# Two decoder layers on one core: the columns of two neighbouring 64-byte lines in turn on TensorE's moving side

## The chip, the cores and the metric

One core of one Trainium2 chip. The time is that of one execution on the device in microseconds; a single core runs, so it is its own slowest.

## The reference

An input x of 256 tokens by 2048 features goes through two pre-norm residual layers in float32. Cut to what matters here:

```
def layer_a(x):                        # latent attention, 16 heads
    h = rms_norm(x, norm_a)
    proj = h @ w_in                    # 2048 -> 512 + 256 + 64 (latents) + 2048 (gate)
    q  = rms_norm(q_lat)  @ w_q_up     # 512 -> 16 x 192
    kv = rms_norm(kv_lat) @ w_kv_up    # 256 -> 16 x (128 + 128)
    o = causal_attention(q, k, v)      # norms on q and k, rotary part of 64
    return x + (o * silu(gate)) @ w_out

def layer_b(x):                        # block attention; with 256 tokens one block of 256
    q, k, v, gate = split(rms_norm(x, norm_b) @ w_in, 4)     # 2048 -> 4 x 2048
    o = causal_attention(rms_norm(q), rms_norm(k), v, alibi) # 16 heads of 128
    return x + (o * silu(gate)) @ w_out
```

## The kernel before

Features lie on the 128 partitions, so `xT` and the residual `xt` are [128, 16 chunks, 256 tokens]. Every dense product is made of three passes in float32r: an operand is cut into a high part (rounded to float32r) and the low rest, and high x high, high x low and low x high are added up in PSUM (`acc`, five banks of 512 columns; attention works in the other three).

Weights stream from DRAM once, in chunks of 128 rows. `W.load` brings a chunk into `wr`; `W.split` makes its parts, `wh` by a ScalarE copy (L124) and `wl` by a VectorE subtraction (L125), 528 splits in all, mostly of 512 columns.

There are two kinds of dense product. `blk_rows` has the tokens as the stationary operand (128 x 128) and the weight as the moving one, 384, 416 or 512 columns: it makes the latents, q, k and v. `blk_cols` has 128 columns of the weight as the stationary operand and all 256 tokens as the moving one: it makes the gates and both output products. Each matmul brings its own load of 128 x 128 stationary values. In attention, `products` makes the scores (`ps_s`), and `s3` in `head_steps` makes the value product (`ps_o`): v stationary, the transposed softmax weights `ph`, `pl`, `p1` moving. Its result times the gate is `og`, cut into `ogh` and `ogl`, the moving side of the output products.

TensorE's work is a written list: `ordered` puts steps of attention between the chunks of dense products by assumed costs, and `chain` keeps TensorE in that order. `run` issues loads and splits four chunks ahead. `xh` and `xl` are the parts of the normed input; `token_scale` makes the norm's factor per token, as a column and (by a product of `ones` with a diagonal tile) along rows; `out_done_a` and `out_done_b` add `acc` to the residual. `flip` transposes q, k and the softmax weights through a DMA: its copies read every second 16-bit word of a tile, or write so.

A row of a tile stands in one partition, 4 bytes for a column. All tiles named here start at a multiple of 64 bytes, so 16 neighbouring columns are one line of 64 bytes in this text.

Of the kernel before, what the change touches and what calls it, by code (L numbers as in the profile page):

```python
"""Two decoder layers (latent attention, then block-sparse attention) on one core.

The dense products run as three float32r passes over operands split exactly into a high and a
low part of 12 bits each. Activations are kept with features on partitions, so that no layer
boundary needs a transpose; weights stream from DRAM once.
"""
# [9 lines left out]
F32 = mybir.dt.float32  # L16
# [5 lines left out]
ALU = mybir.AluOpType  # L22
# [7 lines left out]
WARM = 34  # products of ones while the first loads run  # L30
ACC = 5  # PSUM banks that gather products over the chunks of a weight; attention works in the others
HALF = 3  # chunks of a gate's block that come before the next projections

# tiles for: loaded chunks of weights, their parts; chunks loaded and split ahead
# [3 lines left out]
# For the order of the work, in ns: how long after the end of a piece on the tensor engine what  # L38
# it leaves is ready (norms of the projections of layer a and b, latents, transposed q and k,
# scores, transposed weights of attention of both layers, output of a head), times SLACK; how long  # L40
# a bank is held; and how far pieces of attention lie apart.
# [12 lines left out]
# columns of the packed gains  # L54
# [3 lines left out]
# columns of the packed constants of shape  # L58
# [10 lines left out]
]  # L69


@with_exitstack
def trunk(ctx: ExitStack, tc, xT, gains, cst, w_in_a, w_q_up, w_kv_up, w_out_a, w_in_b, w_out_b, outT):
# [15 lines left out]
    def cut(t, *sizes):  # L89
        """Pieces of a tile, one after the other, each [P, a, b]."""  # L90
        out, at = [], 0
        for a, b in sizes:
            out.append(t[:, at:at + a * b].rearrange("p (a b) -> p a b", a=a))
            at += a * b
        return out
# [4 lines left out]
    # ---------------------------------------------------------------- weights  # L100
    class W:
        """Chunks of 128 rows of a weight, [rows, n] in DRAM, and their high and low parts."""

        def __init__(self, src):
            self.before = lambda: None
            self.src, self.kc, self.n = src, src.shape[0] // P, src.shape[1]
            self.per = max(1, 512 // self.n)
            self.h, self.l = {}, {}
# [10 lines left out]
        def split(self, c):  # L119
            """The parts of the chunks from c on, as many as there are in one step."""  # L120
# [3 lines left out]
            nc.scalar.activation(h, raw, AF.Copy)  # L124
            nc.vector.tensor_tensor(l, raw, h.bitcast(F32), op=ALU.subtract)  # L125
# [3 lines left out]
    # ---------------------------------------------------------------- order of the work  # L129
    class Step:  # L130
        """A piece of work of the tensor engine: about cost ns there, and lag ns from its end until
        what it leaves can be used; needs what some steps leave, and comes after others."""
# [10 lines left out]
    def ordered(main, side):  # L143
        """Steps of main in their order; those of side come between, each as soon as it can and
        one of the three banks that they work in is free."""
# [20 lines left out]
    def chain(ins):  # L166
        """Keep the tensor engine's work in the order in which it is written."""
# [11 lines left out]
    def blk_rows(w, x, done, lag=PB, first=()):  # L179
        """out[token, n] = x.T w for w [K, n]: tokens stationary, the weight streams."""  # L180
# [3 lines left out]
        def go(wt, c, k):  # L184
# [3 lines left out]
            for t in range(2):  # L188
                ts = slice(t * P, (t + 1) * P)
                o = a[t][:, :n]  # L190
                matmul(o, xh[:, k, ts], wt.h[c], start=k == 0, stop=False)
                matmul(o, xh[:, k, ts], wt.l[c], start=False, stop=False)
                matmul(o, xl[:, k, ts], wt.h[c], start=False, stop=k == nk - 1)
# [3 lines left out]
        return _steps(w, go, 6 * (n / 2.4 + 2.5), lag, first)  # L197

    def blk_cols(w, x, done, lag=3000):
        """out[n, token] = w.T x for w [K, n]: the weight stationary, tokens stream."""  # L200
# [3 lines left out]
        def go(wt, c, k):  # L204
# [3 lines left out]
            for s in range(ns):  # L208
# [4 lines left out]
                matmul(o, wt.h[c][:, ws], xh[:, k], start=first, stop=False)  # L213
                matmul(o, wt.h[c][:, ws], xl[:, k], start=False, stop=False)
                matmul(o, wt.l[c][:, ws], xh[:, k], start=False, stop=last)
# [5 lines left out]
    def _steps(w, go, cost, lag, first=()):  # L221
# [3 lines left out]
        for n in list(first) + [nc_w] * nk:  # L225
# [3 lines left out]
            wt = W(w[k0 * P:k1 * P])  # L229
# [21 lines left out]
    # ---------------------------------------------------------------- small things  # L251
    g_sb = one.tile([P, G_END], F32, name="g_sb")
# [18 lines left out]
    def rsqrt(v, n, tag):  # L271
        """v ** -0.5 for positive v: a first guess by its bits, then Newton's steps."""
# [16 lines left out]
    def after(ins, prior):  # L289
        """Work of one engine in this order."""  # L290
# [3 lines left out]
    def sum_squares(ssq, j):  # L294
        """ssq[feature, token] gathers the squares of the two chunks of features j."""
# [9 lines left out]
    def token_scale(ssq, lay, out, needs, more):  # L305
        """1 / rms of each token: as a column per half of the tokens, and along rows."""
# [10 lines left out]
        def g():  # L317
# [4 lines left out]
            matmul(pr[:, :S], ones, d, start=True, stop=True)  # L322
# [6 lines left out]
    # ---------------------------------------------------------------- gates  # L329
# [572 lines left out]
```

## Time and profile before

| | |
|---|---|
| median of 3 runs | 783.33 us (783.16 to 785.5) |
| span of the profiled execution | 780.9 us |
| TensorE busy | 772.9 us, 99% |
| TensorE's weight loads | 717.7 us, 92% |
| VectorE busy | 602.7 us, 77% |
| ScalarE busy | 512.3 us, 66% |
| HBM | 182 GB/s over the span |

The span runs from the first to the last instruction of the profiled execution; the runs' time holds some 2.4 us more. PE is TensorE's matmuls, PEld its loads of stationary operands (they overlap), DVE VectorE, ACT ScalarE. Busy time of PE is not a measure of its speed, since the matmuls are pipelined and their ends are modelled; the distance from one start to the next is.

### The profile page before, as it was taken

How to read it: one execution, taken by the hardware profiler on the slowest of the kernel's cores; microseconds unless marked ns; L12 is line 12 of the kernel's file. 1: busy time of each engine (PE TensorE's matmuls, PEld its weight loads, DVE VectorE, ACT ScalarE, POOL GpSimd, SP SyncE). 2: the span in 40 equal slices, each digit the busy share in tenths (PEclk: the TensorE clock that was granted, in tenths of full speed). 3: DMA queues.
4: the chain of work that ended last, by engine and by line, in shares of the span. 5: the costliest groups of instructions: out<-in, count | busy, mean ns of one | idle time of the engine just before them, and what ended most of it. 6: DMA issues, size and time to landing. Idle time of an engine off the chain costs nothing.

```text
span 780.9 us, 14905 instructions
## 1 busy us (share of the span) xinstructions
PE 772.9 (99%) x5246; PEld 717.7 (92%) x5246; DVE 602.7 (77%) x1470; ACT 512.3 (66%) x1288; POOL 0.2 (0%) x4
## 2 busy tenths in 40 slices
PE   8999999999999999999999999999999999999997
PEld 8999999999999999988889888898889988899997
DVE  7888899999987787766787777786687957887553
ACT  7677898888877665545666556665567655675442
POOL 0000000000000000000000000000000000000000
PEclk9999999999999999999999999999999999999999
DMA  9765656666559766766777667776777677767871
GB/s 305 234 179 174 169 159 182 180 161 158 167 166 249 233 195 188 207 179 183 214 217 175 211 182 222 216 199 191 186 223 208 186 210 194 214 192 213 252 213 61
DMA packets 137979, 153.24 MB, mean 196 GB/s; under 512 B 47280, under 2 KB 94768, under 8 KB 137904
## 3 DMA queue, kind: packets, MB, share of 16 engines
q1 hardware_dynamic: 137760, 152.27, 69.1%
q8 instruction: 41, 0.67, 0.4%
q14 instruction: 34, 0.28, 0.1%
q10 hardware_dynamic: 144, 0.02, 0.0%
HBM read 139.68 MB, written 2.10 MB: 182 GB/s over the span
## 4 chain that ended last, share of the span: by engine, by line
PE 97%; DMA 2%; DVE 1%; SPq 0%; issue 0%; ACT 0%
PE acc L174 89%; PE ps_s L174 4%; PE ps_o L174 2%; PE ps_ta L177 1%; DMA sm<-pz 1%; DMA wr<-w_in_a 1%; DVE wl L125 0%; PE ps_lt L177 0%; DVE xt L825 0%; PE ps_st L174 0%; SPq L449 0%; PE ps_r L174 0%; SPq L113 0%; ACT wh L124 0%; PE ps_kr L177 0%
## 5 line engine op out<-in xcount | busy, mean ns | idle before, releaser
L124 ACT ACTIVATE wh<-wr 128x512 fp32r<-128x512 f32 (+2 forms) x528 | 320.9, 618 | 193.0 <-PE acc L174 120.9
L125 DVE TENSOR_TENSOR wl<-wr,wh 128x512 fp32r<-128x512 f32 (+2 forms) x528 | 348.4, 673 | 109.2 <-ACT wh L124 102.7
L174 PE MATMUL acc<-wh,xh 128*128 128x512 f32 (+1 forms) x448 | 173.8, 388 | 0.8 <-ACT wh L124 0.8
L174 PE MATMUL acc<-wl,xh 128*128 128x512 f32 (+1 forms) x448 | 173.9, 388 | 0.3 <-DVE wl L125 0.3
L174 PE MATMUL acc<-wh,xl 128*128 128x512 f32 (+1 forms) x448 | 174.2, 389 | 0.0
L174 PE MATMUL acc<-xh,wh 128*128 128x256 f32 x512 | 143.8, 281 | 0.0
L174 PE MATMUL acc<-ogh,wh 128*128 128x256 f32 x512 | 142.6, 279 | 0.0
L174 PE MATMUL acc<-xh,wl 128*128 128x256 f32 x512 | 142.3, 278 | 0.2 <-DVE wl L125 0.2
L174 PE MATMUL acc<-xl,wh 128*128 128x256 f32 x512 | 142.3, 278 | 0.0
L174 PE MATMUL acc<-ogl,wh 128*128 128x256 f32 x512 | 141.6, 277 | 0.0
L174 PE MATMUL acc<-ogh,wl 128*128 128x256 f32 x512 | 141.5, 276 | 0.0
L174 PEld LDWEIGHTS acc<-wh,xh 128*128 128x128 f32 x448 | 84.5, 189 | 17.4 <-ACT wh L124 1.5
L174 PEld LDWEIGHTS acc<-wl,xh 128*128 128x128 f32 x448 | 84.4, 188 | 17.4 <-DVE wl L125 0.9
L174 PEld LDWEIGHTS acc<-wh,xl 128*128 128x128 f32 x448 | 84.5, 189 | 15.1
L174 PEld LDWEIGHTS acc<-xl,wh 128*128 128x128 f32 x512 | 96.6, 189 | 0.2
L174 PEld LDWEIGHTS acc<-xh,wl 128*128 128x128 f32 x512 | 96.3, 188 | 0.4 <-DVE wl L125 0.4
L174 PEld LDWEIGHTS acc<-xh,wh 128*128 128x128 f32 x512 | 96.2, 188 | 0.2
L174 PEld LDWEIGHTS acc<-ogh,wh 128*128 128x128 f32 x512 | 96.3, 188 | 0.0
L174 PEld LDWEIGHTS acc<-ogl,wh 128*128 128x128 f32 x512 | 96.2, 188 | 0.0
L174 PEld LDWEIGHTS acc<-ogh,wl 128*128 128x128 f32 x512 | 96.1, 188 | 0.0
L174 PE MATMUL acc<-wh,xt 128*128 128x384 f32 (+1 forms) x192 | 59.5, 367 | 0.0
L174 PEld LDWEIGHTS acc<-wh,xt 128*128 128x128 f32 x192 | 35.5, 188 | 2.1
(150 smaller groups left out, 824.0 us busy)
## 6 DMA issues: line engine op xcount, KB each, us to landing
wr<-w_in_b SPq DMA_DIRECT2D x128, 512.0 KB, 4.2
wr<-w_in_a SPq DMA_DIRECT2D x32, 512.0 KB, 4.6
wr<-w_out_a SPq DMA_DIRECT2D x32, 512.0 KB, 4.5
wr<-w_out_b SPq DMA_DIRECT2D x32, 512.0 KB, 4.5
wr<-w_in_a SPq DMA_DIRECT2D x15, 416.0 KB, 5.0
wr<-w_q_up SPq DMA_DIRECT2D x16, 384.0 KB, 3.4
wr<-w_kv_up SPq DMA_DIRECT2D x8, 512.0 KB, 3.7
xt<-xT SPq DMA_DIRECT2D x4, 512.0 KB, 6.0
```

The lines of the kernel that those rows point to most:

```text
L124: nc.scalar.activation(h, raw, AF.Copy)
L125: nc.vector.tensor_tensor(l, raw, h.bitcast(F32), op=ALU.subtract)
L174: chain(nc.tensor.matmul(*args, skip_group_check=True, **kw))
L177: chain(nc.tensor.transpose(*args))
```

## The change

The moving operand of a product is read in another order. `paired` views 32 columns as two lines of 16 and takes a column of the one and of the other in turn: 0, 16, 1, 17, ... 15, 31, then the next 32. Where the moving operand is a weight (`blk_rows`), its parts are stored so that this order gives the columns as they were: `unpaired` reads `raw` as 0, 2, 4, ... 30, 1, 3, ... 31, so with a step of two columns, and the parts are written line after line. Where the moving operand is the tokens, results come out with the tokens in the paired order and stay so (gates, the row of norm factors, `og`); `ogh`, `ogl` and the residual get the natural order back by an `unpaired` read of `og` and `acc`. The scores' products are left as they are. `g_sb` is allocated with 320 columns instead of 298, which moves all tiles behind it by 64 bytes. No engine has an instruction more or less, and their order is the same.

```
+def paired(v):
+    return v.rearrange("p (g l e) -> p g e l", l=2, e=16)
+def lines(v):
+    return v.rearrange("p (g l e) -> p g l e", l=2, e=16)
+def unpaired(v):
+    return v.rearrange("p (g e l) -> p g l e", l=2, e=16)
...
         def split(self, c):
             m = min(self.per, self.kc - c)
             h, l = self.part("wh", F32R, m, NH, 512), self.part("wl", F32R, m, NH, 512)
             raw = self.raw[:, c:c + m]
-            nc.scalar.activation(h, raw, AF.Copy)
-            nc.vector.tensor_tensor(l, raw, h.bitcast(F32), op=ALU.subtract)
+            ho, lo = h, l
+            if self.moving:
+                assert m == 1
+                raw, ho, lo = unpaired(raw[:, 0]), lines(h[:, 0]), lines(l[:, 0])
+            nc.scalar.activation(ho, raw, AF.Copy)
+            nc.vector.tensor_tensor(lo, raw, ho.bitcast(F32), op=ALU.subtract)
...
     def blk_rows(w, x, done, lag=PB, first=()):
-                matmul(o, xh[:, k, ts], wt.h[c], start=k == 0, stop=False)
-                matmul(o, xh[:, k, ts], wt.l[c], start=False, stop=False)
-                matmul(o, xl[:, k, ts], wt.h[c], start=False, stop=k == nk - 1)
+                matmul(o, xh[:, k, ts], paired(wt.h[c]), start=k == 0, stop=False)
+                matmul(o, xh[:, k, ts], paired(wt.l[c]), start=False, stop=False)
+                matmul(o, xl[:, k, ts], paired(wt.h[c]), start=False, stop=k == nk - 1)
...
     def blk_cols(w, x, done, lag=3000):
-                matmul(o, wt.h[c][:, ws], xh[:, k], start=first, stop=False)
-                matmul(o, wt.h[c][:, ws], xl[:, k], start=False, stop=False)
-                matmul(o, wt.l[c][:, ws], xh[:, k], start=False, stop=last)
+                matmul(o, wt.h[c][:, ws], paired(xh[:, k]), start=first, stop=False)
+                matmul(o, wt.h[c][:, ws], paired(xl[:, k]), start=False, stop=False)
+                matmul(o, wt.l[c][:, ws], paired(xh[:, k]), start=False, stop=last)
...
-    g_sb = one.tile([P, G_END], F32, name="g_sb")
+    g_sb = one.tile([P, 320], F32, name="g_sb")
...
-            matmul(pr[:, :S], ones, d, start=True, stop=True)
+            matmul(pr[:, :S], ones, paired(d), start=True, stop=True)
...
         def s3():
-            matmul(po[:, :S], vh, ph, start=True, stop=False)
-            matmul(po[:, :S], vh, pl, start=False, stop=False)
-            matmul(po[:, :S], vl, ph, start=False, stop=False)
-            matmul(po[:, P:S], v1, p1, start=False, stop=True)
+            matmul(po[:, :S], vh, paired(ph), start=True, stop=False)
+            matmul(po[:, :S], vh, paired(pl), start=False, stop=False)
+            matmul(po[:, :S], vl, paired(ph), start=False, stop=False)
+            matmul(po[:, P:S], v1, paired(p1), start=False, stop=True)
...
-            nc.scalar.activation(ogh[:, h], og, AF.Copy)
-            nc.vector.tensor_tensor(ogl[:, h], og, ogh[:, h].bitcast(F32), op=ALU.subtract)
+            nc.scalar.activation(lines(ogh[:, h]), unpaired(og), AF.Copy)
+            nc.vector.tensor_tensor(lines(ogl[:, h]), unpaired(og), lines(ogh[:, h].bitcast(F32)), op=ALU.subtract)
...
     def out_done_a(j):
-            both = xt[:, c:c + 2].rearrange("p a b -> p (a b)")
-            nc.vector.tensor_tensor(both, a[0], both, op=ALU.add)
+            both = lines(xt[:, c:c + 2].rearrange("p a b -> p (a b)"))
+            nc.vector.tensor_tensor(both, unpaired(a[0]), both, op=ALU.add)
...
     def out_done_b(j):
-                nc.vector.tensor_tensor(y, a[b].rearrange("p (a b) -> p a b", a=2), y, op=ALU.add)
+                both = lines(y.rearrange("p a b -> p (a b)"))
+                nc.vector.tensor_tensor(both, unpaired(a[b]), both, op=ALU.add)
```

## Rows read from the trace of the kernel before

**Rows 1.** The page: busy time of the engines, the clock that TensorE was granted in 40 slices (9 is 90% or more), and the chain that ended last, by engine and by line.

```profile
PE 772.9 (99%) x5246; PEld 717.7 (92%) x5246; DVE 602.7 (77%) x1470; ACT 512.3 (66%) x1288; POOL 0.2 (0%) x4
...
PEclk9999999999999999999999999999999999999999
...
PE 97%; DMA 2%; DVE 1%; SPq 0%; issue 0%; ACT 0%
PE acc L174 89%; PE ps_s L174 4%; PE ps_o L174 2%; PE ps_ta L177 1%; DMA sm<-pz 1%; DMA wr<-w_in_a 1%; DVE wl L125 0%; PE ps_lt L177 0%; DVE xt L825 0%; PE ps_st L174 0%; SPq L449 0%; PE ps_r L174 0%; SPq L113 0%; ACT wh L124 0%; PE ps_kr L177 0%
```

**Rows 2.** Groups of TensorE's matmuls, shapes kept apart: out<-in, the moving columns (128x512 and so on), the count, busy time and mean ns of one. The three passes of a product stand in three rows (`xh,wh`, `xl,wh` and `xh,wl`, and the same with `ogh`), of which one each is shown.

```profile
L174 PE MATMUL acc<-wh,xl 128*128 128x512 f32 x384 | 151.6, 395 | 0.0
...
L174 PE MATMUL acc<-xh,wh 128*128 128x256 f32 x512 | 143.8, 281 | 0.0
...
L174 PE MATMUL acc<-wh,xt 128*128 128x384 f32 x128 | 36.7, 346 | 0.0
L174 PE MATMUL acc<-wh,xt 128*128 128x512 f32 x64 | 23.2, 408 | 0.0
L174 PE MATMUL acc<-wh,xh 128*128 128x416 f32 x64 | 23.1, 361 | 0.8 <-ACT wh L124 0.8
...
L174 PE MATMUL ps_o<-pl,vh 128*128 128x256 f32 x32 | 9.1, 286 | 0.1
```

**Rows 3.** The chain that ended last, in order of time: start in us, length in us, what, and how many instructions in a row. The first is a stretch of the latents (416 columns), the second of gates and the third of output products (256 columns), the fourth is the end of the program.

```profile
9.86 29.46 PE acc L174 x155
...
134.56 9.89 PE acc L174 x84
...
261.22 61.89 PE acc L174 x546
...
776.29 1.37 DVE xt L825 x2
```

**Rows 4.** The timeline of a row product of layer b, start and length in us: the first and the last of ten matmuls of 512 columns in a row.

```profile
449.74 0.39 PE L174 MATMUL acc<-wh,xl 128*128 128x512 f32 x1
...
451.80 0.39 PE L174 MATMUL acc<-wh,xl 128*128 128x512 f32 x1
```

**Rows 5.** The same some 50 us earlier, again the first and the last of ten.

```profile
399.75 0.40 PE L174 MATMUL acc<-wh,xl 128*128 128x512 f32 x1
...
401.85 0.40 PE L174 MATMUL acc<-wh,xl 128*128 128x512 f32 x1
```

**Rows 6.** The timeline of TensorE in the first gate block of layer b: the first and the last of 38 matmuls of 256 columns, the float32 product of the norm factors in two rows, and the first and last of ten matmuls behind it.

```profile
327.26 0.28 PE L174 MATMUL acc<-xl,wh 128*128 128x256 f32 x1
...
331.45 0.28 PE L174 MATMUL acc<-xh,wl 128*128 128x256 f32 x1
331.57 0.59 PE L174 MATMUL ps_r<-diag,ones 128*128 128x256 f32 x2
...
332.12 0.28 PE L174 MATMUL acc<-xl,wh 128*128 128x256 f32 x1
...
333.18 0.28 PE L174 MATMUL acc<-xl,wh 128*128 128x256 f32 x1
```

**Rows 7.** Four float32 transposes on TensorE in the timeline, the length of one of them, and the loads of weights by form (count, busy us and mean ns of one).

```profile
78.91 0.60 PE L177 MATMUL ps_ta<-c_sb,tok 128*128 128x128 f32 x4
...
L177 PE MATMUL ps_ta<-c_sb,tok x64: 270/272/273, 78.9 to 233.5; 128*128 128x128 f32 x64
...
L174 PEld LDWEIGHTS acc<-xl,wh 128*128 128x128 f32 x512 | 96.6, 189 | 0.2
...
L177 PEld LDWEIGHTS ps_ta<-c_sb,tok 128*128 128x128 f32 x64 | 7.5, 141 | 0.1
```

**Rows 8.** Groups of VectorE, shapes kept apart: splits of 512 columns, a subtraction of 256, the copy of `flip` that reads with a step, and the residual sums of both layers.

```profile
L125 DVE TENSOR_TENSOR wl<-wr,wh 128x512 fp32r<-128x512 f32 x464 | 313.4, 687 | 105.4 <-ACT wh L124 99.1 <-PE ps_s L174 2.7 <-PE acc L174 1.8
...
L411 DVE TENSOR_TENSOR pl<-pz,ph 128x256 fp32r<-128x256 f32 x32 | 13.3, 419 | 0.0
...
L378 DVE COPY flip<-tok 128x1024 uint16<-128x1024 uint16 x16 | 10.3, 685 | 0.0
...
L691 DVE TENSOR_TENSOR xt<-acc,xt 128x512 f32<-128x512 f32 x8 | 5.5, 688 | 0.5
...
L825 DVE TENSOR_TENSOR xt<-acc,xt 128x512 f32<-128x512 f32 x8 | 5.2, 684 | 4.9 <-PE acc L174 4.9
```

**Rows 9.** Groups of ScalarE, shapes kept apart: splits of 512 columns, the copy of `flip` that reads with a step, and a copy of 128 columns.

```profile
L124 ACT ACTIVATE wh<-wr 128x512 fp32r<-128x512 f32 x464 | 287.6, 629 | 174.2 <-PE acc L174 106.8 <-DVE wl L125 61.6 <-ACT wh L124 2.4
...
L378 ACT COPY pz<-sm 128x768 uint16<-128x768 uint16 x16 | 13.2, 825 | 2.3 <-DVE sm L402 1.9 <-ACT wh L124 0.3
...
L413 ACT COPY p<-pz 128x128 f32<-128x128 f32 x32 | 9.4, 294 | 0.0
```

**Rows 10.** Busy time of the engines by stage: the stretch in us, then us busy of PE, PEld, DVE, ACT and POOL with their counts, the granted clock, the share of the DMA engines and GB/s. The first three lie in layer a, the fourth in a row product of layer b.

```profile
50.00:100.00 50.00, 50.00 (x388) 48.78 (x386) 43.45 (x131) 37.55 (x118) 0.00 (x0) 1.00 0.59 157
100.00:150.00 50.00, 49.76 (x371) 48.44 (x370) 46.62 (x141) 42.80 (x139) 0.00 (x0) 1.00 0.64 175
...
200.00:250.00 50.00, 50.00 (x412) 49.37 (x411) 43.41 (x141) 38.71 (x117) 0.00 (x0) 1.00 0.62 177
...
430.00:505.00 75.00, 75.00 (x370) 63.14 (x368) 56.84 (x118) 45.45 (x104) 0.00 (x0) 1.00 0.72 210
```

More of the change, by code (lines that the diff above doesn't have):

```diff
@@ L101, in trunk, with __init__ @@
     class W:
-        def __init__(self, src):
+        def __init__(self, src, moving):
             self.before = lambda: None
+            self.moving = moving
             self.src, self.kc, self.n = src, src.shape[0] // P, src.shape[1]
@@ L190, in go @@
                 o = a[t][:, :n]
-                matmul(o, xh[:, k, ts], wt.h[c], start=k == 0, stop=False)
-                matmul(o, xh[:, k, ts], wt.l[c], start=False, stop=False)
-                matmul(o, xl[:, k, ts], wt.h[c], start=False, stop=k == nk - 1)
+                matmul(o, xh[:, k, ts], paired(wt.h[c]), start=k == 0, stop=False)
+                matmul(o, xh[:, k, ts], paired(wt.l[c]), start=False, stop=False)
+                matmul(o, xl[:, k, ts], paired(wt.h[c]), start=False, stop=k == nk - 1)
             if k == nk - 1:
                 done([a[t][:, :n] for t in range(2)])
-        return _steps(w, go, 6 * (n / 2.4 + 2.5), lag, first)
+        return _steps(w, go, 6 * (n / 2.4 + 2.5), lag, first, True)
     def blk_cols(w, x, done, lag=3000):
@@ L219, in blk_cols, with _steps @@
         return _steps(w, go, 3 * ns * 109, lag)
-    def _steps(w, go, cost, lag, first=()):
+    def _steps(w, go, cost, lag, first=(), moving=False):
         out, nc_w = [], 1024 // w.shape[1]
@@ L228, in _steps @@
                 break
-            wt = W(w[k0 * P:k1 * P])
+            wt = W(w[k0 * P:k1 * P], moving)
             for k in range(k0, k1):
@@ L458, in rest @@
         with tc.issue_after(lat1[0].w[0].dma):
-            nc.sync.dma_start(g_sb[:, G_QN:], gains[:, G_QN:])
+            nc.sync.dma_start(g_sb[:, G_QN:G_END], gains[:, G_QN:])
             nc.sync.dma_start(c_sb, cst[:, :C_COS])
```

## The prediction

> **What bounds the kernel now.** I read the page first. TensorE is busy for 772.9 of 780.9 us, at a granted clock of 1.0 (the 2.4 GHz level) in every slice, and 97% of the chain that ended last is TensorE, 89% of it the products into `acc` [rows 1]. The reader should see that nobody is waited for: the question is how long one matmul keeps TensorE, not what it waits for. The busy column doesn't tell that, since matmuls overlap (a 256-column one is shown with 281 ns [rows 2], but the next starts long before its end). The pace is the distance between two starts, so I read the chain and the timeline for stretches of equal matmuls.
>
> In the chain 546 products of 256 columns take 61.89 us, 113.4 ns each; in another stretch 84 take 9.89 us, 117.7 ns; 155 products of 416 columns take 29.46 us, 190.1 ns [rows 3]. In the timeline nine steps of 512 columns take 2.06 us (228.9 ns) in one place [rows 4] and 2.10 us (233.3 ns) in another [rows 5]. At one column per cycle of 2.4 GHz 256 columns would last 106.7 ns, 416 columns 173.3 and 512 columns 213.3. So they cost 272 cycles for 256, or 16 too many: one for each 16 columns, that is for each 64 bytes of a row. The slow stretches have 26 too many in 256, the wide products 37 or 48 in 512. No width shows a fixed cost per matmul beside this share.
>
> The same matmuls change pace in the middle of a gate block: 37 steps from 327.26 to 331.45 us take 113.2 ns each, then two float32 matmuls come between, and the nine behind them take 117.8 ns [rows 6]. Tiles, widths and addresses of the moving side are the same on both sides of that point. So a part of the loss depends on how the moving read meets something else in time, and the other reader next to it is the load of the next weights.
>
> **The change, part by part.**
>
> *Moving reads.* All products into `acc` and the value products read the moving side in another order; sequence and count of every engine's instructions stay. There are 6 x 512 + 96 = 3168 products of 256 columns, 3 x 384 + 96 = 1248 of 512, 192 of 384 and 192 of 416 [rows 2]. Over the whole trace, from each start to the next of the same width, they take on the mean 114.3, 230.0, 173.4 and 188.4 ns (about a fifth of the 256 run at the slow pace: 0.8 x 113.4 + 0.2 x 117.7 = 114.3). Together that is 362 + 287 + 33 + 36 = 718 us, all but 55 us of TensorE's time. No TensorE row of before reads with a step, so the price must be bounded from both sides.
>
> Below: the extra cycle falls away and nothing takes its place. 512 columns then cost 213.3 ns, 384 cost 160.0, 416 cost 173.3. For 256 the load of the next 128 weights may set the pace. Its shortest spacing is uncertain: four float32 transposes with a load each stand 109 ns apart (from 78.91, the group lasts 0.60 us with the last one's 272 ns, so 0.33 us for three steps), although their loads are shown with 141 ns and those of the products with 189 ns [rows 7]. I take 109 ns. If only the regular cycle goes and the irregular part stays, 512 columns cost 230.0 - 13.3 = 216.7 ns. I take the middle, 215, and for 384 and 416 likewise 161.5 and 175. The gain: 3168 x 5.3 = 16.8 us, 1248 x 15.0 = 18.7, 192 x 11.9 = 2.3, 192 x 13.4 = 2.6. Sum 40.4 us. The bounds of this case are 43.1 us (all at one column per cycle but the 256 at 109) and 34.2 us (the 512, 384 and 416 keep their irregular part and lose only a cycle in 16 columns, and the 256 come to 110). Above: the alternation makes it worse; that is a rival below, since a cost per change of line is what the rows show, and the change raises the number of changes sixteenfold.
>
> [...]
>
> *Storing weights' parts.* 272 of 528 splits (those of the row products: 2 x 16 for the latents, 8 x 6 for the heads of layer a, 4 x 3 x 16 in layer b) read `raw` with a step of 8 bytes. Now a split of 512 takes 629 ns on ScalarE and 687 ns on VectorE [rows 8, 9]. The nearest rows with a step are the copies of `flip`, which read every second 16-bit word: 768 of them take ScalarE 825 ns, where its unstepped rows (294 ns for 128, 629 for 512, so 0.872 ns per element) give 852; VectorE reads 1024 in 685 ns. A step shows no surcharge there, so I take nothing. The other end is twice the time per element: VectorE's slope is (687 - 419) / 256 = 1.05 ns, so 0.54 us more per split. That is a rival too.
>
> *Tokens.* `ogh` and `ogl` (32 x 256 each), and `xt` at the end of both output products (16 x 512, 688 and 684 ns now [rows 8]), are read with the step. VectorE and ScalarE have room beside TensorE; only the last two `xt` sums lie in the open, 1.37 us at 776.29 [rows 3]. Twice their per-element time would cost 1.1 us; I take nothing. The wider `g_sb` moves every tile behind it by 64 bytes, which keeps the pairs whole and costs nothing in time.
>
> *What takes back some of it.* From 100 to 150 us VectorE is busy 46.62 of 50 us, from 50 to 100 and 200 to 250 some 43.4 [rows 10]. TensorE faster by 5% there means VectorE at up to 98%, and some waits for it. The attention's way through VectorE, ScalarE and the transposing DMA keeps its length, so the two places where output products wait for the last heads lose a little. I allow 2 us for all of this.
>
> The sum: 780.9 - 40.4 + 2 = 742.5 us of span. The median of the runs, 783.3, lies 2.4 us over the span of the profiled execution, so **745 us**.
>
> **Rivals.**
>
> *The weight load holds the 256-column products* at 113 ns, and only the wide ones gain: 18.7 + 2.3 + 2.6 = 23.6 us less, some 1 us lost, 761 us. For it: a load is shown with 189 ns, and no product into `acc` follows another closer than 113. Against it: the 512-column products lose at least as much per column [rows 4, 5], and there a load has twice the time. Chance 0.13.
>
> *No change.* The cycle in 16 isn't tied to the address at all but to the stream of float32 columns; then the order of reading moves nothing, 783 us. For it: the pace changes with time and not with the tile [rows 6]. Chance 0.12.
>
> *Every change of line costs its cycle.* Now one is paid per 16 columns; in turn, every column enters another line than the one before. 256 columns would take 512 cycles, 213.3 ns, and 512 take 426.7: 3168 x 99 + 1248 x 196.7 + 192 x (146.6 + 158.3) = 618 us more, 1400 us. It decides as soon as a change costs more than a sixteenth of a cycle. Against it: the pace change at 331 us speaks for two readers that meet, and spreading a reader over two lines halves what it wants of each. [...] Chance 0.14.
>
> *VectorE pays for the step.* With 0.54 us more per split of 512 the row products of layer b turn over to VectorE: from 430 to 505 us it has 56.84 busy of 75 [rows 10], and 75 / 1.373 = 54.6 splits (six products of 228.9 ns each) add 29 us, 86 us instead of 75. Four such stages (192 splits) give 39 us more; layer a, with VectorE nearly full, some 10 more; the 256-column products still give 17 back: about 815 us. It decides from (75 - 56.84) / 54.6 = 0.33 us per split. Together with cases where the new order collides more with the weight loads and costs up to 5%, chance 0.11.
>
> **How the numbers follow.** The forecast has 0.50, its own range 735 to 757. What a measurement of this kernel can tell from no change is about 0.3%, 2.3 us. Faster: 0.50 + 0.13 = 0.63; within 0.3%: 0.12; slower: 0.14 + 0.11 = 0.25. A range from 734 to 825 leaves out the doubling (0.14) and a little at both ends.
>
> **What would show it.** Right: starts of `acc` products of 256 columns about 109 ns apart, of 512 about 215, while the score products (`ps_s`, which keep their order) stay at 113 to 118; splits still at 629 and 687 ns; TensorE still over 97% of the chain. If 256 stays at 113 and 512 falls, the weight load is the limit. If both stay, the address was not the cause. The prediction would be wrong outright if matmuls get longer, or if ScalarE's or VectorE's splits pass about 1.0 us and TensorE begins to wait for `wl`.

## The result

The changed kernel takes 762.61 us (761.27 to 762.8 in four runs), before took 783.28 us beside it: a ratio of 0.9725, interval 0.9709 to 0.9741. That is 20.7 us less, about half of the 38 us forecast.

The page of the changed kernel, the rows that answer to [rows 1] (line numbers are those of the changed file; L199 is L174 of before, L149 and L150 the splits of L124 and L125):

```profile
PE 749.5 (99%) x5246; PEld 708.8 (93%) x5246; DVE 599.5 (79%) x1470; ACT 521.1 (68%) x1288; POOL 0.2 (0%) x4
...
PE 63%; DMA 2%; DVE 2%; ACT 1%; issue 0%; DVEq 0%; ACTq 0%
PE acc L199 61%; PE ps_o L199 2%; PE ps_s L199 1%; DMA sm<-pz 1%; DMA tok<-flip 1%; DVE wl L150 1%; ACT wh L149 0%; ACT sqa L768 0%; DMA c_sb<-cst 0%; DVE xt L852 0%; DVE tok L774 0%; DVE flip L404 0%; PE ps_r L199 0%; DVE sm L428 0%; DVE sm L421 0%
```

TensorE is still busy 99% of the span, 23 us less of it. The shares of the chain listed add up to 68% of the span only, so it is no full account here; what it shows is that it now runs at places through transposing DMAs and VectorE. The pace is the thing to look at first: the chain's longest stretch of output products, which answers to the third line of [rows 3], and ten products of 512 columns in layer b, which answer to [rows 4, 5] (start and length in us).

```profile
258.43 60.97 PE acc L199 x546
```

```profile
439.95 0.38 PE L199 MATMUL acc<-wh,xl 128*128 128x512 f32 x1
...
441.90 0.38 PE L199 MATMUL acc<-wh,xl 128*128 128x512 f32 x1
```

The 256-column products now stand 111.7 ns apart (60.97 / 546), the 512-column ones some 216 (nine steps in 1.95 us as printed; 215.8 over the 1,186 pairs of the trace that nothing parts). Over the whole trace, without the pairs that a wait or a piece of attention parts, the mean distance between products of one width went from 114.3 to 111.7 ns for 256 columns, from 230.0 to 215.8 for 512, from 173.4 to 162.6 for 384 and from 188.4 to 175.8 for 416. From 384 to 512 columns that is now (215.8 - 162.6) / 128 = 0.416 ns for each column, so 2.4 columns per ns; a cycle below is such a step, 0.417 ns. Nearly every such pair has exactly this distance: the two paces of before, and their change in mid-block, are gone. By count, from unrounded means, this is 8.4 + 17.7 + 2.1 + 2.4 = 30.6 us. The span fell by 20.0 us, so 10.6 us came back elsewhere. The waits of TensorE and of its weight loads, before (the first two lines) and after, in us in total, times, longest:

```profile
PE ps_o L174 <- ACT ph L410: 1.4, 1, 1.4
...
PEld acc L174 <- DVE wl L125: 1.3, 3, 0.4
...
PE ps_o L199 <- ACT ph L436: 2.1, 1, 2.1
PE acc L199 <- DVE wl L150: 2.0, 5, 0.8
...
PEld acc L199 <- DVE wl L150: 7.4, 19, 1.0
```

Loads of weights waited 7.4 us for VectorE's part `wl`, where before it was 1.3 us in 3 waits. That is 6.1 us more. Not all of it delays TensorE, since a load can wait while the product in front of it still runs: by the starts of the products behind these loads, counted over both traces, some 5 us of the 10.6 were lost there. The stretch around 254 us shows another part, by the granted clock (the last three columns are clock, DMA share and GB/s):

```profile
252.00:254.00 2.00, 1.51 (x6) 1.32 (x7) 2.00 (x5) 1.72 (x6) 0.00 (x0) 0.69 1.09 347
254.00:256.00 2.00, 2.00 (x11) 2.00 (x11) 1.26 (x3) 0.91 (x3) 0.00 (x0) 0.50 1.12 356
256.00:258.00 2.00, 2.00 (x20) 2.00 (x19) 1.32 (x3) 1.18 (x3) 0.00 (x0) 0.96 0.74 236
```

After a wait of 2.1 us for `ph` TensorE was granted a clock of 0.5 through the whole middle stretch and parts of its neighbours: eleven products stand 190 to 215 instead of 111.7 ns apart, 1.1 us in all. Before, the same wait was 1.4 us and the clock stayed at 1.0. This part belongs to the profiled execution: of the four runs two have a mean clock of 0.998, as this one, and two have 1.000. One group of TensorE completes the list, before and after, mean ns of one:

```profile
L174 PE MATMUL ps_o<-p,v 128*128 128x128 f32 x64 | 12.3, 273 | 0.0
...
L199 PE MATMUL ps_o<-p,v 128*128 128x128 f32 x64 | 14.2, 304 | 0.0
```

The float32 part of the value product (`p1`, whose buffers show as p) is 304 ns long now, 273 before: 1.9 us more over its 64 records. The sum of what came back: some 5 for `wl`, 1.9 for float32, 1.1 for the clock, 0.7 each for `ph` and for a wait of the scores for VectorE, some 0.5 for latents, about 10 us of the 10.6 sought.

The splits, shapes kept apart, which answer to the first lines of [rows 8, 9]:

```profile
L149 ACT ACTIVATE wh<-wr 128x512 fp32r<-128x512 f32 x464 | 296.2, 656 | 135.9 <-PE acc L199 125.4 <-DMA wr<-w_out_b 2.7 <-DVE rs_y L305 2.4
...
L150 DVE TENSOR_TENSOR wl<-wr,wh 128x512 fp32r<-128x512 f32 x464 | 311.3, 689 | 85.8 <-ACT wh L149 82.3 <-PE ps_s L199 1.4
```

VectorE pays nothing for the step (687 before). ScalarE pays a little: 208 of these 464 read with the step, so they take 629 + (656 - 629) x 464 / 208 = 689 ns, 60 ns more each. ScalarE waits 136 us in front of these splits, so it has the time.

### The profile page after: what moved, and what is told of

The parts are those of the page before. It is cut to its first block, busy times and chain, and to the rows that moved or that the text cites. A ratio compares the mean times of both kernels' runs of the same rounds, so it can differ in the third digit from the quotient of the medians.

```text
span 760.9 us, 14905 instructions
## 1 busy us (share of the span) xinstructions
PE 749.5 (99%) x5246; PEld 708.8 (93%) x5246; DVE 599.5 (79%) x1470; ACT 521.1 (68%) x1288; POOL 0.2 (0%) x4
## 4 chain that ended last, share of the span: by engine, by line
PE 63%; DMA 2%; DVE 2%; ACT 1%; issue 0%; DVEq 0%; ACTq 0%
PE acc L199 61%; PE ps_o L199 2%; PE ps_s L199 1%; DMA sm<-pz 1%; DMA tok<-flip 1%; DVE wl L150 1%; ACT wh L149 0%; ACT sqa L768 0%; DMA c_sb<-cst 0%; DVE xt L852 0%; DVE tok L774 0%; DVE flip L404 0%; PE ps_r L199 0%; DVE sm L428 0%; DVE sm L421 0%
## 5 line engine op out<-in xcount | busy, mean ns | idle before, releaser
L149 ACT ACTIVATE wh<-wr 128x512 fp32r<-128x512 f32 (+2 forms) x528 | 331.8, 646 | 147.8 <-PE acc L199 132.9
L150 DVE TENSOR_TENSOR wl<-wr,wh 128x512 fp32r<-128x512 f32 (+2 forms) x528 | 346.2, 675 | 88.8 <-ACT wh L149 84.8
L199 PE MATMUL acc<-wh,xh 128*128 128x512 f32 (+1 forms) x448 | 169.1, 377 | 0.8 <-ACT wh L149 0.8
L199 PE MATMUL acc<-wl,xh 128*128 128x512 f32 (+1 forms) x448 | 168.8, 377 | 1.0 <-DVE wl L150 0.9
L199 PE MATMUL acc<-wh,xl 128*128 128x512 f32 (+1 forms) x448 | 167.6, 374 | 0.0
L199 PE MATMUL acc<-ogh,wh 128*128 128x256 f32 x512 | 142.6, 278 | 0.0
L199 PE MATMUL acc<-xh,wh 128*128 128x256 f32 x512 | 142.3, 278 | 0.0
L199 PE MATMUL acc<-xh,wl 128*128 128x256 f32 x512 | 141.3, 276 | 1.0 <-DVE wl L150 0.8
L199 PE MATMUL acc<-ogl,wh 128*128 128x256 f32 x512 | 141.4, 276 | 0.0
L199 PE MATMUL acc<-ogh,wl 128*128 128x256 f32 x512 | 141.3, 276 | 0.0
L199 PE MATMUL acc<-xl,wh 128*128 128x256 f32 x512 | 140.8, 275 | 0.0
L199 PEld LDWEIGHTS acc<-xh,wl 128*128 128x128 f32 x512 | 98.3, 192 | 1.9 <-DVE wl L150 1.9
L199 PEld LDWEIGHTS acc<-ogh,wl 128*128 128x128 f32 x512 | 98.8, 193 | 0.2 <-DVE wl L150 0.2
L199 PEld LDWEIGHTS acc<-ogl,wh 128*128 128x128 f32 x512 | 98.8, 193 | 0.1
L199 PEld LDWEIGHTS acc<-ogh,wh 128*128 128x128 f32 x512 | 98.8, 193 | 0.0
L199 PEld LDWEIGHTS acc<-xl,wh 128*128 128x128 f32 x512 | 98.2, 192 | 0.3
L199 PEld LDWEIGHTS acc<-xh,wh 128*128 128x128 f32 x512 | 98.2, 192 | 0.3
L199 PEld LDWEIGHTS acc<-wl,xh 128*128 128x128 f32 x448 | 84.9, 190 | 14.4 <-DVE wl L150 4.5
L199 PEld LDWEIGHTS acc<-wh,xh 128*128 128x128 f32 x448 | 85.0, 190 | 11.5 <-ACT wh L149 1.4
L199 PEld LDWEIGHTS acc<-wh,xl 128*128 128x128 f32 x448 | 85.0, 190 | 10.1
L199 PE MATMUL acc<-wh,xt 128*128 128x384 f32 (+1 forms) x192 | 57.5, 357 | 0.0
L199 PEld LDWEIGHTS acc<-wh,xt 128*128 128x128 f32 x192 | 35.1, 189 | 1.3
```

The source lines that it names most:

```text
L149: nc.scalar.activation(ho, raw, AF.Copy)
L150: nc.vector.tensor_tensor(lo, raw, ho.bitcast(F32), op=ALU.subtract)
L199: chain(nc.tensor.matmul(*args, skip_group_check=True, **kw))
```

## The experiments

### Which orders of reading are fast

Two kernels run the changed kernel and then series of 24 matmuls on tiles at hand, so that one clock and one trace compare the orders. The first list:

```
+    flat = xh.rearrange("p c s -> p (c s)")
+    def turns(v, l, e):
+        return v.rearrange("p (g l e) -> p g e l", l=l, e=e)
+    bench("aNat", flat[:, :256], 256)
+    bench("aPair", turns(flat[:, :256], 2, 16), 256)
+    bench("aHalf", turns(flat[:, :256], 2, 8), 256)
+    bench("aQuart", turns(flat[:, :256], 2, 4), 256)
+    bench("aSkip", turns(flat[:, :256], 2, 32), 256)
+    bench("aFour", turns(flat[:, :256], 4, 16), 256)
...
+    bench("bFar", turns(flat[:, :512], 2, 256), 512)
+    bench("bShift", flat[:, 8:520], 512)
+    bench("cStep", flat[:, 0:512:2], 256)
+    bench("cStepq", flat[:, 0:1024:4], 256)
+    bench("cLine", flat[:, 0:4096:16], 256)
+    bench("eNat", flat[:, :256], 256, 64)
+    bench("ePair", turns(flat[:, :256], 2, 16), 256, 64)
+    bench("fNat", ident, 128, P, ident)
+    bench("fPair", turns(ident, 2, 16), 128, P, ident)
```

> The changed kernel with twenty series of 24 matmuls behind its last product, on tiles that lie in SBUF by then; their results go nowhere. Read from it: the distance from one start to the next in each series. Theory A (one 64-byte line gives float32 columns a little too slowly, two neighbouring lines in turn give one column per cycle plus some 6 cycles per matmul; the load of 128 weights takes about 111.7 ns): 256 columns natural (aNat) 113 to 118 ns, paired (aPair) 111.7, turns within one line (aHalf, 2 x 32 bytes; aQuart, 2 x 16 bytes) as aNat, four lines in turn (aFour) 111.7; 512 columns natural (bNat) 226 to 234, paired (bPair) 215.8, within a line (bHalf) as bNat, four lines (bFour) 215.8. With only 64 weight columns to load, ePair falls to about 109 and eNat stays at 113 or above. Lines an even number apart (aSkip, bSkip: two lines; bFar: sixteen): 111.7 and 215.8 if any two lines do, as natural or slower if neighbours differ in something that lines two apart share. Rival B (any order but the natural one gains): aHalf and bHalf fall too. Rival C (each entered line costs one cycle): columns with a step of two (cStep) 120 ns, of four (cStepq) 133 ns, one column per line (cLine) 213 ns; under A these stay near 111.7 where neighbouring lines come in turn (cLine). Float32 products of 128 columns (fPair against fNat): about 25 ns longer per record in the paired order, as in the value product p1 of the changed kernel.

The timeline of the series, start and length in us (a series' pace is the distance to the next one's start, over 24; the float32 ones have two records for a matmul):

```profile
754.40 3.04 PE L199 MATMUL aNat<-xh 128*128 128x256 f32 x24
757.28 2.84 PE L199 MATMUL aPair<-xh 128*128 128x256 f32 x24
759.96 2.84 PE L199 MATMUL aHalf<-xh 128*128 128x256 f32 x24
762.64 2.84 PE L199 MATMUL aQuart<-xh 128*128 128x256 f32 x24
765.32 2.84 PE L199 MATMUL aSkip<-xh 128*128 128x256 f32 x24
768.00 3.41 PE L199 MATMUL aFour<-xh 128*128 128x256 f32 x24
771.25 5.62 PE L199 MATMUL bNat<-xh 128*128 128x512 f32 x24
776.70 5.34 PE L199 MATMUL bPair<-xh 128*128 128x512 f32 x24
781.88 5.34 PE L199 MATMUL bHalf<-xh 128*128 128x512 f32 x24
787.06 5.34 PE L199 MATMUL bSkip<-xh 128*128 128x512 f32 x24
792.24 6.62 PE L199 MATMUL bFour<-xh 128*128 128x512 f32 x24
798.69 5.34 PE L199 MATMUL bFar<-xh 128*128 128x512 f32 x24
803.87 5.76 PE L199 MATMUL bShift<-xh 128*128 128x512 f32 x24
809.47 5.69 PE L199 MATMUL cStep<-xh 128*128 128x256 f32 x24
814.98 5.78 PE L199 MATMUL cStepq<-xh 128*128 128x256 f32 x24
820.58 5.46 PE L199 MATMUL cLine<-xh 128*128 128x256 f32 x24
825.86 2.92 PE L199 MATMUL eNat<-xh 128*64 128x256 f32 x24
828.61 2.78 PE L199 MATMUL ePair<-xh 128*64 128x256 f32 x24
831.23 5.52 PE L199 MATMUL fNat<-c_sb 128*128 128x128 f32 x48
836.59 6.63 PE L199 MATMUL fPair<-c_sb 128*128 128x128 f32 x47
```

Natural order: 120.0 ns for 256 columns, 227.1 for 512. Two neighbouring lines in turn: 111.7 and 215.8. But so do two halves of one line (aHalf, bHalf), two quarters (aQuart), lines two apart (aSkip, bSkip) and lines sixteen apart (bFar), to the hundredth of a microsecond. So the part of theory A that speaks of two *lines* falls: it takes two places in turn, wherever they lie in these series (16 to 1024 bytes apart). Four places in turn are worse than none (135.4 and 268.8 ns). Rival B, any order but the natural one, was right for the halves and wrong for four places. Rival C falls at cStep: it enters 32 lines where the natural order enters 16, and costs 229.6 ns instead of the 120 forecast, and one column per line (cLine, 220.0) is no dearer. Each fixed step here (2, 4 and 16 columns: 229.6, 233.3 and 220.0 ns) costs a little over two cycles per column. ePair points at the load: with 64 weight columns 109.2 ns, so 128 columns of weights seem to hold 256 moving ones at 111.7. That the load is too long, and not that the two reads disturb each other, is an inference: the wide products bring the same loads and keep their 6 cycles (215.8 ns, 518 cycles for 512 columns). fPair costs 138 ns per record, fNat 111.7.

The second list asks whether the distance's parity or pieces of 16 bytes explain it:

```
+    bench("nLine", flat[:, 16:272], 256)     # nHalf from 8, nQuart from 4, nOne from 1
...
+    bench("tTwo", turns(flat[:, :256], 2, 2), 256)
+    bench("tShift", turns(flat[:, 8:264], 2, 16), 256)
+    bench("tOdd", turns(flat[:, :240], 2, 15), 240)
+    bench("sTwo", flat[:, 0:512:2], 256)     # sThree, sFive, sFifteen: steps of 3, 5, 15
...
+    bench("wStep", turns(flat[:, :256], 2, 16), 256, P, lambda s: flat[:, 1024:1280:2])
```

> A second list of series behind the changed kernel's last product, 24 matmuls each, results going nowhere; all but the w series with 64 weight columns, where a load does not set the pace (109.2 ns for 256 columns in the first list). The first list showed 111.7 ns for any two places in turn (8, 32, 128, 1024 bytes apart or two neighbouring lines), 135.6 for four lines in turn, 226 to 233 for steps of 2, 4 and 16 columns, 114 to 120 for the natural order. Theory P (a row is delivered in two halves, even and odd 4-byte words, each a column every second cycle, with a short buffer): steps of 3, 5 and 15 columns (sThree, sFive, sFifteen) alternate even and odd and stay near 109 to 120 ns, while a step of 2 (sTwo) stays near 230; two places 15 columns apart (tOdd, 240 columns) cost 102 to 110 ns; 0,2,1,3 (tTwo) 109. Theory L (a matmul reads whole lines or pieces of 16 bytes, and needs two columns from each): sThree, sFive and sFifteen cost some 213 to 235 ns as sTwo does. The natural order at other offsets (nLine 64 bytes, nHalf 32, nQuart 16, nOne 4): if its loss comes from entered lines, 113 to 118 everywhere, nHalf, nQuart and nOne one line more; if from how it meets the weight read, no order by offset. With 128 weight columns: wNat 113 to 120, wPair 111.7; wStep (weights read with a step of two columns, tokens paired): 111.7 if the load is not slowed by its read order, 200 or more if it is.

```profile
754.63 2.90 PE L199 MATMUL nZero<-xh 128*64 128x256 f32 x24
757.36 2.97 PE L199 MATMUL nLine<-xh 128*64 128x256 f32 x24
760.17 3.02 PE L199 MATMUL nHalf<-xh 128*64 128x256 f32 x24
763.02 2.97 PE L199 MATMUL nQuart<-xh 128*64 128x256 f32 x24
765.82 3.02 PE L199 MATMUL nOne<-xh 128*64 128x256 f32 x24
768.68 2.89 PE L199 MATMUL tTwo<-xh 128*64 128x256 f32 x24
771.41 2.78 PE L199 MATMUL tShift<-xh 128*64 128x256 f32 x24
774.03 2.63 PE L199 MATMUL tOdd<-xh 128*64 128x240 f32 x24
776.49 5.61 PE L199 MATMUL sTwo<-xh 128*64 128x256 f32 x24
781.92 5.62 PE L199 MATMUL sThree<-xh 128*64 128x256 f32 x24
787.36 5.66 PE L199 MATMUL sFive<-xh 128*64 128x256 f32 x24
792.83 6.02 PE L199 MATMUL sFifteen<-xh 128*64 128x256 f32 x24
798.66 3.05 PE L199 MATMUL wNat<-xh 128*128 128x256 f32 x24
801.55 2.85 PE L199 MATMUL wPair<-xh 128*128 128x256 f32 x24
804.23 3.04 PE L199 MATMUL wStep<-xh 128*128 128x256 f32 x24
```

Steps of 3, 5 and 15 columns cost 226.7, 227.9 and 242.9 ns, where a step of 2 costs 226.2: theory P falls. Theory L forecast 213 to 235 ns for these steps, and two of the three lie there, but it does not stand as it was put, since aHalf (111.7 ns) and tOdd (240 columns in 102.5 ns, 246 cycles) alternate between pieces 32 and 60 bytes apart without that cost. Turns of two columns each (tTwo) are as slow as the natural order, 113.8. The natural order costs 113.8, 117.1, 118.8, 116.7 and 119.2 ns at five offsets, and 113.8 (nZero) or 120.4 (wNat) on the same data with 64 or 128 weight columns: its price moved with the offset and with the weights that were loaded beside it. The paired order costs 109.2 ns at two offsets (ePair, tShift). With weights read with a step of two columns (wStep) the products stand 120 ns apart instead of 111.7, which neither forecast had. Why turns come faster than the natural order is not settled by these runs.

### Each part alone

Row products alone: `paired` and `unpaired` stay on the weights and go from the tokens, the value products, `og` and the residual sums.

```
-                matmul(o, wt.h[c][:, ws], paired(xh[:, k]), start=first, stop=False)
+                matmul(o, wt.h[c][:, ws], xh[:, k], start=first, stop=False)
...
```

> One part alone: only the row products read their moving weight in turns (weights' parts stored to match); tokens are read in their natural order everywhere. Theory (the pace gain of 512, 416 and 384 columns is 17.7 + 2.4 + 2.1 = 22 us, of which later waits for VectorE take some 3 us back): about 764 to 766 us. Rival (the two parts only pay together, or the tokens' part is what pays): 775 us or more.

766.84 us (763.1 to 770.26), ratio 0.9776 (0.9734 to 0.9818) to 784.95 of before beside it. 512 columns stand 215.8 ns apart, 256 columns 114.5. In the chain:

```profile
261.51 61.90 PE acc L199 x546
```

That is 113.4 ns each, as in [rows 3]. The tokens alone:

```
-                matmul(o, xh[:, k, ts], paired(wt.h[c]), start=k == 0, stop=False)
+                matmul(o, xh[:, k, ts], wt.h[c], start=k == 0, stop=False)
...
-        return _steps(w, go, 6 * (n / 2.4 + 2.5), lag, first, True)
+        return _steps(w, go, 6 * (n / 2.4 + 2.5), lag, first)
```

> The other part alone: the tokens are read in turns in the column products and the value products, the weights' parts stay as they were. Theory (the pace gain of 256 columns is 114.3 - 111.7 = 2.6 ns times 3168 = 8.4 us; float32 p1 costs 1.6 us more): about 776 us, and 512 columns stay at 226 to 234 ns. Rival (the load of weights sets the 256-column pace anyway and the gain there comes from something else): 782 us or more.

777.53 us (775.72 to 779.29), ratio 0.9912 (0.9885 to 0.9939). The 256 stand at 111.7, the 512 at 229.0 ns. The tokens came out at what their pace gives (8.4 us less 1.9 for float32). The row products gave 4 us less than their 22.2, about the 3 expected: loads waited 6.1 us for `wl` there, and 1.7 us with the tokens alone, so these waits came with the faster row products. The parts are worth 18.1 and 7.4 us against 22.1 us for both (next run): the difference of 3 us lies within the intervals.

### Where the pairs lie

```
-    g_sb = one.tile([P, 320], F32, name="g_sb")
+    g_sb = one.tile([P, G_END], F32, name="g_sb")
```

> The changed kernel with g_sb at its old 298 columns, so that all tiles behind it lie 64 bytes lower (token tiles at an odd multiple of 64 bytes, weights' parts at an even one). Theory (only that two neighbouring lines come in turn matters, not which is first): the same as the changed kernel, 762.6 us within 1.5. Rival (the move of the tiles is part of the gain): 766 us or more, or another pace of the products.

762.87 us (760.72 to 763.2), ratio 0.9721 (0.9693 to 0.9748), the same paces. The wider `g_sb` does nothing. Then the whole kernel with turns within one line:

```
 def paired(v):
-    return v.rearrange("p (g l e) -> p g e l", l=2, e=16)
+    return v.rearrange("p (g l e) -> p g e l", l=2, e=4)
...
```

> The changed kernel, but the turns are taken between the two halves of 32 bytes (columns 0, 4, 1, 5, 2, 6, 3, 7), so within one 64-byte line; weights' parts and tokens are stored to match. Theory after the two lists (any two places in turn, each with at least four columns in a row, give one column per cycle): the same as the changed kernel, 762.6 us within 2, the products at 215.8 and 111.7 ns. Rival (in the kernel, with loads and copies around, neighbouring 64-byte lines matter): 770 to 783 us.

760.8 us (759.92 to 762.0), ratio 0.9714 (0.9688 to 0.974), 215.8 and 111.7 ns. So what the lists showed holds in the kernel: neighbouring 64-byte lines are not what pays.

### What the float32 products pay

```
-            matmul(po[:, P:S], v1, paired(p1), start=False, stop=True)
+            matmul(po[:, P:S], v1, p1, start=False, stop=True)
...
-            nc.scalar.copy(p1, pz[:, S:])
+            nc.scalar.copy(p1.rearrange("p (g e l) -> p g e l", l=2, e=16), paired(pz[:, S:]))
```

> The changed kernel, but the two float32 moving operands (p1 of the value product and the diagonal tile) are stored in turns and read as they lie. The first list showed 137.8 ns for a float32 record read in turns and 111.7 for one read as it lies, 26 ns. Theory (that is 26 ns times 2 records times 32 heads = 1.7 us, all on TensorE's path): 761 us against 762.6. Rival (the copies to store p1 cost ScalarE what TensorE gains, or TensorE waits for other things there): 762.6 or more.

760.58 us (759.91 to 761.17), ratio 0.9705 (0.9684 to 0.9726). The p1 records are back:

```profile
L199 PE MATMUL ps_o<-p,v 128*128 128x128 f32 x64 | 12.4, 275 | 0.0
```

1.8 us less there and 2.0 in the median: the theory held, though the intervals of this variant and of the changed kernel touch. It is the fastest kernel tried, level with the turns within a line.

### Where the rest came back

Four attempts at the waits of TensorE, and two of them together. Five blocks of output products in front of layer a's last heads:

```
-    for b in outs_a[:4]:
+    for b in outs_a[:5]:
...
```

> The changed kernel, but five blocks of layer a's output product instead of four give their first twelve chunks before the last heads are needed: some 8 us more of TensorE's work in front of the wait of 2.3 us for ph at 252 us and of the lower clock behind it (11 matmuls at 213 instead of 112 ns, 1.1 us). Theory (the wait and the clock cost 3.4 us there, and the work moved ahead covers it): 759 us. Rival (the work is the same, and the blocks behind then wait for their own splits): 762 us or more.

761.87 us (759.58 to 763.32), ratio 0.9723 (0.9697 to 0.9748); the wait for `ph` is where it was, 2.2 us. By the code, the order of steps by assumed costs writes the value product when it expects it to be ready, however much other work there is; that this is why more work in front did not help is not shown. The transposes in two steps each:

```
-        front(planes(b), words(a))
-        nc.sync.dma_start_transpose(a.bitcast(U16).rearrange("p (c t) -> p c t", t=P), b.bitcast(U16))
-        nc.vector.tensor_copy(words(b), planes(a))
+        front(planes(b), words(a))
+        nc.sync.dma_start_transpose(a.bitcast(U16).rearrange("p (c t) -> p c t", t=P), b.bitcast(U16))
+        def back():
+            nc.vector.tensor_copy(words(b), planes(a))
+        return back
...
+        b0 = Step(s2, 0, BACK, [a])
+        b = Step(s2_back, 0, lag - BACK, [b0])
```

> The changed kernel, but each transposition through the DMA is two steps: copy and DMA in the first, the copy back and what follows in a second one at least 3 us later in the written order, so that VectorE does not stand still for the DMA with the splits of weights queued behind. Theory (of the 31 us that VectorE waits for these DMAs, the part that makes TensorE wait for wl, some 3 to 5 us of the 7.4 us of such waits, goes away): 758 to 760 us. Rival (the waits for wl come from VectorE's load before the splits, not from the DMA): 762 us; or the later use of the transposed tiles makes TensorE wait for them, over 763.

762.22 us (761.98 to 762.28), ratio 0.9726 (0.9706 to 0.9746): no gain, and VectorE still waits for the DMAs of q and k, 17.2 us where it was 17.6, and 10.7 instead of 13.5 us for those of the softmax weights. TensorE's wait for `ph` fell to 0.9 us. The waits of the loads for `wl` grew:

```profile
PEld acc L200 <- DVE wl L151: 8.8, 17, 1.2
```

So this edit gains nothing, but it left most of VectorE's standing still in place, and does not decide between theory and rival. Splits written five chunks ahead, on top of x_stored:

```
-NL, NS = 4, 4
+NL, NS = 4, 5
```

> The variant with float32 operands stored in turns (x_stored, 760.6 us), and the splits written five chunks ahead of TensorE instead of four, so that a split stands in front of the norms of a projection on VectorE instead of behind them. Theory (TensorE's 6.9 us of waits for wl come from VectorE's work that stands before the split: 1.0 us at 116 us, 0.3 us at 138, 160, 182 and 205 us, 0.9 us at 463 us): at least half of them go, 756 to 758 us. Rival (there are five tiles for the parts, so the fifth split waits on ScalarE for the matmul that frees its tile and holds up attention's work behind it): 760 us or more.

769.54 us (766.84 to 770.4), ratio 0.9817 (0.9795 to 0.9839), 9 us slower than x_stored:

```profile
PEld acc L199 <- DVE wl L150: 15.9, 33, 1.4
```

The theory falls; the waits more than doubled (6.9 us in x_stored). The rival's reason does not show either: ScalarE's splits wait 124.9 us for TensorE here and 133.6 in x_stored, while VectorE's wait for the transposed softmax weights grew from 13.9 to 26.5 us. A longer time from a head's transposition to its value product in layer a:

```
-... S1, S2A, S2B, S3 = 9000, 6000, 5000, 3000, 10000, 4800, 6000, 9000, 3000
+... S1, S2A, S2B, S3 = 9000, 6000, 5000, 3000, 10000, 4800, 8000, 9000, 3000
```

> The variant with float32 operands stored in turns (x_stored, 760.6 us), and the written order counts on 8 us instead of 6 from a head's transposition to its value product in layer a (times 1.3). Theory (the wait of 2.3 us for ph at 252 us and what hangs on it is there because the value product was written too early, not for lack of other work): the wait goes, 757 to 758 us. Rival (another step of attention is late in its place): 760 us or more.

767.08 us (766.33 to 768.91), ratio 0.9793 (0.977 to 0.9817). The wait for `ph` fell from 2.2 to 0.7 us, but in its place TensorE waits for `ogh`, and its loads for `wl` 10.5 us:

```profile
PE acc L199 <- ACT ogh L453: 2.5, 2, 1.8
...
PEld acc L199 <- DVE wl L150: 10.5, 19, 2.0
```

Both edits together:

> x_ahead and x_lag together. Theory (two separate causes): their gains add up, 754 to 756 us. Rival (they take the same time back): no better than the better one of them.

773.24 us (771.48 to 775.32), ratio 0.9872 (0.9849 to 0.9895): the losses nearly add up (12.7 us over x_stored, 9.0 and 6.5 alone). So that TensorE waits for VectorE's splits is measured, and x_stored bears out what float32 costs; the clock's part is read from one execution; which order of VectorE's work would take the 6 us of waits away stays open.

## Why the prediction was right and where it failed

The direction and the place were right: TensorE's pace bounds the kernel, the changed read gives nearly one column per cycle (518 cycles for 512 columns), no engine becomes the bound, and 762.6 us lies in the range of 734 to 825. It lies outside the likeliest case's own range of 735 to 757, and the stated range holds it because it was drawn to take in the rivals too. Point by point:

- *Wide products.* Forecast 215, 161.5 and 175 ns, measured 215.8, 162.6 and 175.8; 22.2 us gained of 23.6 forecast. The extra that came and went with time disappeared altogether, and what took its place is 6 cycles per matmul, which no row of before shows: nearly every pair of the changed kernel shows 518 cycles for 512 columns; 256 take 262 (109.2 ns) in the series with 64 weight columns and 268 (111.7 ns) in the kernel, with 128. Nor does a row of before show the 2.4 columns per ns that the forecast counts its cycles by; the 0.416 ns per column of the changed kernel bear them out.
- *256-column products.* This is the term that was mis-sized. I took 109 ns from the spacing of transposes [rows 7]; they stand at 111.7, so 8.4 us came instead of 16.8. The series with 64 weight columns points at the reason: 109.2 ns there, 111.7 with 128. The rival of the weight load forecast 761 us, close to the result, but by a load that leaves nothing to gain at 113 ns, and with 1 us lost; that 30.6 us less 10.6 end near its 23.6 less 1 is chance. The load seems to set the pace, 2.5 ns above the read with 64 weight columns and 2.6 below the old mean of 114.3. The spacing of transposes was a poor row for it, as their loads are shown with 141 ns and the products' with 189.
- *What comes back.* I allowed 2 us, 10.6 came. VectorE at up to 93% in layer a [rows 10] was named as the place, but priced by the busy share alone. Some 5 us were lost to waits for `wl` in 19 places, in layer b too, where VectorE is busy three quarters of the time. The 2.4 us from span to time were mis-read too: in the runs that show both (762.7 and 760.9, 783.3 and 781.5) it is 1.8.
- *Float32 products.* Their moving side changed too, and the sum had no term for it: 1.9 us.
- *Storing the parts.* VectorE pays nothing (689 ns a split, 687 before), as taken from the copies of `flip` [rows 8]; ScalarE pays 60 ns a split and hides it, since it waits 136 us in front of them. The rival in which VectorE pays is out. The stepped reads of the tokens cost nothing in the open, as taken: the last two sums last 1.36 us, 1.37 before.
- *The doubling.* A cost for each change of line is out: aPair changes line with every column, and at 111.7 ns none of its width and weights is faster. A fixed step does cost, but one of 2 columns (8 bytes, 229.6 ns) no less than one of 16 (220.0 ns).
- *The reason.* I read the cycle in 16 columns as one for each 64-byte line and half believed in two readers that meet. The first is wrong as a cause of the gain: turns within one line do the same. For the second, the natural order's dependence on the weights loaded beside it (113.8 and 120.4 ns) speaks, no more; why turns pay stays open.

## What to carry to other kernels

Where float32r products are paced by TensorE, compare the distance between starts with columns times 0.417 ns. If it is 6 to 10% longer (here 113.4 to 117.7 ns for 256 columns, 228.9 and 233.3 for 512), try reading the moving side from two places in turn, each with four or more consecutive columns (111.7 and 215.8 ns here, but 113.8 with two columns each), and leave the result in a plain order; keep float32 operands in the order in which they lie (111.7 ns a record of 128 columns, 138 in turns), and keep fixed steps (2 to 16 columns here, 220 to 243 ns for 256) off the moving side. When the bounding engine gets faster, price what the next one must deliver by its waits at single places, not by its busy share: here a sixth of the pace gained (some 5 of 30.6 us) went there.

## What the runs showed of the hardware

- Moving reads of float32r from two places in turn stood columns times 0.417 ns plus 6 cycles apart: 215.8 ns for 512, 162.6 for 384 and 175.8 for 416 in the changed kernel, 215.8 for 512 with the places 32, 64, 128 or 1024 bytes apart (m_orders) and 16 bytes apart (e_quart), 102.5 for 240 with 60 bytes (m_orders2, 64 weight columns). In natural order 256 columns took 113 to 120 ns; four places in turn 135 ns (m_orders); fixed steps of 2, 3, 4, 5, 15 and 16 columns 220 to 243 ns (both lists).
- 256 moving columns read in turns stood 111.7 ns apart with 128 float32r weight columns and 109.2 with 64 (m_orders). With weights read with a step of two columns: 120 ns (m_orders2).
- A float32 moving read (128 columns) went the other way: 111.7 ns per record in natural order, 138 in turns (m_orders).
- After one wait of 2.1 us TensorE's granted clock was 0.5 for a stretch of the changed kernel. In that place 24 products of 256 columns took 4.34 us (181 ns each) in e_rows, after 2.3 us, and 3.60 us (150 ns each) in e_tokens, where the paces are 114.5 and 111.7. After 2.2 us in x_stored, x_five and e_quart (all with a mean clock of 1.000) it stayed up.
